# Value heads straight from the products: which operand is stationary in a two-layer diffusion step

## The chip, the cores and the metric

The kernel runs on one core of one Trainium2 chip. The metric is the time of one execution on the device in microseconds. TensorE is called PE in the profile, its weight loads PEld, VectorE DVE, ScalarE ACT, GpSimd POOL and the engine that issues most transfers SP.

## The reference, cut to what matters

Two trunk layers are applied to two groups of 128 tokens, context and latent, with model width 2048. Layer 0 mixes with eight latent (MLA) heads and eight grouped-query heads, layer 1 with eight differential heads; each layer ends in a gated feed-forward network. The change touches how the values of two kinds of heads are made:

```python
kv = (ckv_all @ w_kv_up).reshape(b, s, MLA_HEADS, MLA_NOPE_DIM + MLA_V_DIM)   # s = 128, or 128 cached + 128
...
va = kv[..., MLA_NOPE_DIM:]
out_a = softmax_attention(jnp.concatenate([qa_nope, qa_rope], axis=-1), ka, va, MLA_SCALE)
...
proj = h @ w_in                                                                # layer 1
v = proj[..., 2 * nq:].reshape(b, t, DIFF_HEADS, 2 * HEAD_DIM)
```

A latent head has 128 key and 128 value columns out of a latent of 512, for 384 token rows in all (context, cache, latent tokens). A differential head has two queries, two keys and one value of 256 columns, out of 2048 inputs, for 256 token rows; its cached values come from an input. All arithmetic is float32.

## The kernel before, in words

Activations lie with features on partitions and tokens along the free axis: `x` and the modulated input `hx` are tiles of 16 blocks of 128 features, each with 256 tokens (128 context, then 128 latent). Each input of a product is split into a high part rounded to float32r and the rest as a low part; `split` (L219 to L221) does that with a copy on ACT and a subtraction on DVE. A product is three matmuls for each block of 128 inputs: weight high by input high, weight high by input low, weight low by input high. In `gemm` (L304 to L318) the weight block, 128 inputs by 128 outputs, is the stationary operand, and the tokens move past it, 256 at once (384 in the latent heads' keys and values). The result has output features on partitions. It stands in one of three PSUM banks of the tag `acc`.

Weights come from memory in tiles of 1 MB named `raw`, 16 blocks of 128x128, three of them in turn. `Weights.chunk` (L255 to L281) loads a tile when its blocks have run out, splits each half of it into `wh` and `wl` of 1024 columns (four buffers each), and gives out the blocks of one chunk, that is of 128 outputs.

Attention needs the values the other way round, with tokens on partitions. So a value chunk is copied out of PSUM by ACT, transposed on PE by a matmul with the identity into a PSUM tile of the tag `att` (three of them in turn), and copied by ACT into the tile that the attention reads. For the differential heads that is L914 to L923 in `project`: two chunks, copied to `dev`, four transposes, two copies into `dv`. For the latent heads it is `vt` (L847), three transposes (L854) and `vm` (L855, L856) in `values_and_head`.

The order of the work. The tile framework orders each engine's queue by a simulated timeline, starting from the program's order; instructions marked with `keep_in_program_order` stay where they are. Attention is written as generators: `start` runs one to its first `yield`, and each `pump` runs every waiting one a step further (L147 to L158). `pump` also brings in the work on the modulation of later layers: rows of `w_ada`, as matmuls on PE (L427) or as sums on DVE (L404), at a rate for each stage. The first three products of a stage are made by `first_three` (L283 to L302); the next products take the entries of `todo`, the rest of one unit of modulation rows.

In the latent and grouped-query stage the loop at L825 goes over eight heads; every second one makes three query chunks for two heads. Each head starts a grouped-query head, makes a key chunk and a value chunk, and starts the latent head. In the differential stage `project` (L891 to L925) makes for each of eight heads two query chunks, two key chunks with rotation (L903 to L912; L909 on DVE and L905 to L907 on ACT read the accumulator), and two value chunks; `attend` (L927 to L976) then does scores (L934), softmax, transposes of the weights (L607), the weighted sum (L952 to L954), a norm (L958 to L968) and the turning back (L973). The output projection follows at L983.

## Time and profile before

| what | value |
|---|---|
| median of three runs | 2375.56 us (2375.53 to 2375.99) |
| the profiled execution's own time | 2375.77 us |
| its span, first to last instruction | 2374.0 us |
| mean granted TensorE clock | 0.989 |
| PE busy | 2315.6 us, 98% of the span |
| latent and grouped-query heads | about 223 to 375 us |
| differential heads | about 1208 to 1543 us |

The page of the profile has the busy time of each engine, the chain of work that ended last, and groups of instructions by source line. A row of a group reads: line, engine, operation, what it writes and reads, shape, count, then busy time in us and the mean of one in ns, and the idle time of the engine before it. A row of the timeline begins with the start in us and the duration; where instructions are merged, xN tells how many. Durations of matmuls overlap, so what one costs in a stream is read from the distance of the starts.

### The profile page before, as it was taken

How to read it: one execution, taken by the hardware profiler on the slowest of the kernel's cores; microseconds unless marked ns; L12 is line 12 of the kernel's file. 1: busy time of each engine (PE TensorE's matmuls, PEld its weight loads, DVE VectorE, ACT ScalarE, POOL GpSimd, SP SyncE). 2: the span in 40 equal slices, each digit the busy share in tenths (PEclk: the TensorE clock that was granted, in tenths of full speed). 3: DMA queues.
4: the chain of work that ended last, by engine and by line, in shares of the span. 5: the costliest groups of instructions: out<-in, count | busy, mean ns of one | idle time of the engine just before them, and what ended most of it. 6: DMA issues, size and time to landing. Idle time of an engine off the chain costs nothing.

```text
span 2374.0 us, 47094 instructions
## 1 busy us (share of the span) xinstructions
PE 2315.6 (98%) x19626; PEld 2196.9 (93%) x19626; DVE 1799.1 (76%) x2677; ACT 1172.7 (49%) x1855; POOL 136.6 (6%) x132
## 2 busy tenths in 40 slices
PE   8899999999999999999999999998999999999997
PEld 6778868799999999999989999897999999999997
DVE  2667544479999999999968889799899755666654
ACT  4345544365554345554465555445555434555542
POOL 0001001110000000001220000022000000000011
PEclk9999999999999999999999999998999999999998
DMA  9886677877767876777767788776677555555553
GB/s 378 353 342 241 238 266 300 309 275 266 261 252 281 296 277 251 265 264 268 300 229 256 267 315 290 269 288 240 247 260 260 207 195 195 196 194 192 192 192 120
DMA packets 92405, 610.81 MB, mean 257 GB/s; under 512 B 9952, under 2 KB 17824, under 8 KB 20512
## 3 DMA queue, kind: packets, MB, share of 16 engines
q1 hardware_dynamic: 92192, 607.80, 69.6%
q8 instruction: 154, 2.52, 0.4%
q14 instruction: 59, 0.48, 0.1%
HBM read 603.01 MB, written 4.75 MB: 256 GB/s over the span
## 4 chain that ended last, share of the span: by engine, by line
PE 95%; DVE 2%; DMA 1%; issue 1%; ACT 1%; POOL 0%; POOLq 0%; DVEq 0%; ACTq 0%
PE acc L313 28%; PE acc L317 28%; PE acc L314 28%; PE ada L427 3%; DMA araw<-w_ada 1%; PE att L617 1%; PE acc L300 1%; PE acc L299 1%; PE acc L301 1%; PE misc L427 0%; PE att L934 0%; PE att L607 0%; DVE wl L221 0%; PE ada L340 0%; PE ada L376 0%
## 5 line engine op out<-in xcount | busy, mean ns | idle before, releaser
L220 ACT CAST wh<-raw 128x1024 fp32r<-128x1024 f32 (+1 forms) x788 | 794.0, 1013 | 943.1 <-PE acc L314 775.7
L221 DVE TENSOR_TENSOR wl<-raw,wh 128x1024 fp32r<-128x1024 f32 (+1 forms) x788 | 923.0, 1186 | 343.8 <-ACT wh L220 324.5
L313 PE MATMUL acc<-hx,wh 128*128 128x256 f32 x4064 | 1131.6, 279 | 9.7 <-ACT wh L220 4.2
L317 PE MATMUL acc<-hx,wl 128*128 128x256 f32 x4064 | 1127.8, 278 | 0.7 <-DVE wl L221 0.7
L314 PE MATMUL acc<-hx,wh 128*128 128x256 f32 x4064 | 1128.4, 278 | 0.0
L313 PEld LDWEIGHTS acc<-hx,wh 128*128 128x128 f32 x4064 | 764.7, 188 | 35.7 <-issue 13.3
L317 PEld LDWEIGHTS acc<-hx,wl 128*128 128x128 f32 x4064 | 765.0, 188 | 8.9 <-issue 6.7
L314 PEld LDWEIGHTS acc<-hx,wh 128*128 128x128 f32 x4064 | 765.3, 188 | 7.4 <-issue 6.9
L404 DVE CUSTOM_DVE_ANT_0 junk<-araw,condb 128x2048 f32<-128x2048 f32 (+1 forms) x184 | 424.8, 2309 | 1.1 <-DMA araw<-w_ada 1.1
L314 PE MATMUL acc<-g,wh 128*128 128x256 f32 x1408 | 388.3, 276 | 0.0
L317 PE MATMUL acc<-g,wl 128*128 128x256 f32 x1408 | 388.0, 276 | 0.0
L313 PE MATMUL acc<-g,wh 128*128 128x256 f32 x1408 | 387.8, 276 | 0.0
L314 PEld LDWEIGHTS acc<-g,wh 128*128 128x128 f32 x1408 | 264.3, 188 | 0.0
L317 PEld LDWEIGHTS acc<-g,wl 128*128 128x128 f32 x1408 | 264.2, 188 | 0.0
L313 PEld LDWEIGHTS acc<-g,wh 128*128 128x128 f32 x1408 | 264.1, 188 | 0.0
L175 POOL TENSOR_TENSOR sqacc<-sqacc,sq 128x256 f32<-128x256 f32 x62 | 80.7, 1302 | 1584.3 <-issue 1290.8
L1011 ACT ACTIVATE cv<-acc,convw 128x256 f32<-128x256 f32 x176 | 98.3, 559 | 2.8 <-PE acc L301 2.8
L569 DVE SCALAR_TENSOR_TENSOR x<-acc,mod,x 128x128 f32<-128x128 f32 x192 | 58.0, 343 | 49.2 <-PE acc L317 49.2
L427 PE MATMUL ada<-araw,condw 128*32 128x512 f32 x608 | 83.2, 624 | 6.0 <-DMA araw<-w_ada 5.0
L1017 DVE SCALAR_TENSOR_TENSOR cv<-acc,convw,cv 128x254 f32<-128x254 f32 x176 | 84.4, 480 | 3.7
L1014 DVE SCALAR_TENSOR_TENSOR cv<-acc,convw,cv 128x254 f32<-128x254 f32 x176 | 83.7, 476 | 2.2 <-ACT cv L1011 2.2
L313 PE MATMUL acc<-oall,wh 128*128 128x256 f32 x208 | 58.4, 281 | 2.3 <-DVE x L569 2.3
(229 smaller groups left out, 1789.8 us busy)
## 6 DMA issues: line engine op xcount, KB each, us to landing
araw<-w_ada SPq DMA_DIRECT2D x186, 1024.0 KB, 5.4
raw<-w_up SPq DMA_DIRECT2D x176, 1024.0 KB, 4.8
raw<-w_down SPq DMA_DIRECT2D x88, 1024.0 KB, 4.8
raw<-w_in_c SPq DMA_DIRECT2D x48, 1024.0 KB, 5.5
raw<-w_in_ab SPq DMA_DIRECT2D x19, 1024.0 KB, 7.1
raw<-w_out_ab SPq DMA_DIRECT2D x16, 1024.0 KB, 7.1
raw<-w_out_c SPq DMA_DIRECT2D x16, 1024.0 KB, 5.3
raw<-w_ada SPq DMA_DIRECT2D x6, 1024.0 KB, 10.8
```

The source lines that it names most:

```text
L175: pool.tensor_tensor(out=st["acc"], in0=st["acc"], in1=sq, op=ALU.add)
L220: pin(act.copy(out_hi, src))
L221: pin(dve.tensor_tensor(out=out_lo, in0=src, in1=out_hi.bitcast(F32), op=ALU.subtract))
L313: fixed(pe.matmul(ps[:, :n], wh, xh(k), start=(i == 0), stop=False))
L314: fixed(pe.matmul(ps[:, :n], wh, xl(k), start=False, stop=False))
L317: fixed(pe.matmul(ps[:, :n], wl, xh(k), start=False, stop=(i == last)))
L404: tc.keep_in_program_order(dve.tensor_tensor_reduce(out=junk, in0=raw, in1=condb[:, c].rearrange("p (g n) -> p g n", g=4), scale=1.0, scal ...
L427: i = pe.matmul(ada["ps"][32 * g:32 * g + 32, :], condw[:, 4 * t + g, :], raw[:, g], start=(t == 0), stop=(t == 3), skip_group_check=True)
L569: dve.scalar_tensor_tensor(out=x[:, c, s], in0=ps[:, s], scalar=mod[:, l, 3 * which + 2, c, g:g + 1], in1=x[:, c, s], op0=ALU.mult, op1=AL ...
L1011: pin(act.activation(y, ps, AF.Identity, scale=cw[:, 1, m:m + 1], bias=cw[:, 3, m:m + 1]))
L1014: pin(dve.scalar_tensor_tensor(out=y3[:, :, 1:], in0=p3[:, :, :T - 1], scalar=cw[:, 0, m:m + 1], in1=y3[:, :, 1:], op0=ALU.mult, op1=ALU.add))
L1017: pin(dve.scalar_tensor_tensor(out=y3[:, :, :T - 1], in0=p3[:, :, 1:], scalar=cw[:, 2, m:m + 1], in1=y3[:, :, :T - 1], op0=ALU.mult, op1=A ...
```

## The change

`by_token` makes a product with the tokens stationary: the 128x128 block of the input, high or low part, is loaded as weights, and two chunks' weights, 256 columns, move past it. The result has tokens on partitions, which is what attention reads, and goes with one copy into the value tile.

For the differential heads, the two value chunks of a head are interleaved in memory so that each block of 128 inputs has its 256 columns side by side; `pairs` splits half a tile at a time, and two accumulators, one for each group of tokens, are filled together. For the latent heads, two heads go together: the tile of four chunks holds the two key chunks in its first half and the two value chunks, interleaved, in its second; the values of the pair come after both key chunks, in three runs over the three blocks of tokens. The two latent heads of a pair start after that, one `pump` apart. `values_and_head` is gone, and `vm` holds two heads.

```diff
--- before.py
+++ after.py
@@ -274,11 +274,34 @@
                     at = lo % 8 * P
                     wh, wl = wh_[:, at:at + w], wl_[:, at:at + w]
                     split(wh, wl, raw[:, lo * P:hi * P])
+                    self.pieces = (wh, wl)
                     for b in range(hi - lo):
                         s = slice(b * P, (b + 1) * P)
                         self.blocks.append((wh[:, s], wl[:, s]))
             out, self.blocks = self.blocks[:self.nblk], self.blocks[self.nblk:]
             return out
+
+        def pairs(self, lo):
+
+            if lo == 0:
+                self.raw = self.load()
+            wh = T_(wpool, [P, 1024], "wh", F32R, bufs=4)
+            wl = T_(wpool, [P, 1024], "wl", F32R, bufs=4)
+            split(wh, wl, self.raw[:, lo * P:(lo + 8) * P])
+            return wh, wl
+
+    def by_token(pieces, xs, outs, first, last):
+
+        wh, wl = pieces
+        n = len(xs)
+        for k in range(n):
+            a, b = first and k == 0, last and k == n - 1
+            s = slice(2 * k * P, (2 * k + 2) * P)
+            for (hi, lo), ps in zip(xs[k], outs):
+                pe.matmul(ps, hi, wh[:, s], start=a, stop=False)
+                pe.matmul(ps, lo, wh[:, s], start=False, stop=False)
+            for (hi, lo), ps in zip(xs[k], outs):
+                pe.matmul(ps, hi, wl[:, s], start=False, stop=b)
 
     def first_three(W, xh, xl, order, mid=None, fixed=False):
 
@@ -818,46 +841,47 @@
                 def mla(h, qnh, qrh, knh, vh):
                     half = slice(64 * (h % 2), 64 * (h % 2) + 64)
                     return head_ab(hp, [(qnh, knh), (qrh[half], kr[half])], rsm,
-                                   lambda b: vh[:, b], o, h)
+                                   lambda b: vh[:, b, h % 2], o, h)
 
                 flush()
                 start(gqa_query(0))
-                for h in range(8):
-                    if h % 2 == 0:
-                        for i in range(2):
-                            ps = gemm(WQ.chunk(), qh, qlo)
-                            qn[h + i] = T_(hp, [P, NT], "qn", bufs=4)
-                            act.copy(qn[h + i], ps)
-                            pump(RATE["heads"])
+                blocks = [slice(b * T, (b + 1) * T) for b in range(3)]
+                tokens = [[[(kv_in[:, k, 0, b], kv_in[:, k, 1, b])] for k in range(4)] for b in blocks]
+                for h in range(0, 8, 2):
+                    for i in range(2):
                         ps = gemm(WQ.chunk(), qh, qlo)
-                        ev = T_(tmp, [P, NT], "nt", bufs=4)
-                        act.copy(ev, ps)
-                        qr = T_(hp, [P, NT], "qr", bufs=2)
-                        act.copy(qr[:, 0:T], ev[:, 0:T])
-                        rope(qr[:, None, T:], ev[:, None, T:], 1, 32, "rcm", "rsm")
+                        qn[i] = T_(hp, [P, NT], "qn", bufs=4)
+                        act.copy(qn[i], ps)
                         pump(RATE["heads"])
-                    if h < 7:
-                        start(gqa_query(h + 1))
-                    start(gqa(h))
-                    ps = gemm(WK.chunk(), kh, klo, 3 * T)
-                    kn = T_(hp, [P, 3 * T], "kn", bufs=2)
-                    act.copy(kn, ps)
+                    ps = gemm(WQ.chunk(), qh, qlo)
+                    ev = T_(tmp, [P, NT], "nt", bufs=4)
+                    act.copy(ev, ps)
+                    qr = T_(hp, [P, NT], "qr", bufs=2)
+                    act.copy(qr[:, 0:T], ev[:, 0:T])
+                    rope(qr[:, None, T:], ev[:, None, T:], 1, 32, "rcm", "rsm")
                     pump(RATE["heads"])
-                    ps = gemm(WK.chunk(), kh, klo, 3 * T)
-                    vt = T_(hp, [P, 3 * T], "vt", bufs=2)
-                    act.copy(vt, ps)
+                    kn = []
+                    for i in range(2):
+                        if h + i < 7:
+                            start(gqa_query(h + i + 1))
+                        start(gqa(h + i))
+                        ps = gemm(WK.chunk(), kh, klo, 3 * T)
+                        kn.append(T_(hp, [P, 3 * T], "kn", bufs=2))
+                        act.copy(kn[i], ps)
+                        pump(RATE["heads"])
+                    wide = WK.pieces
+                    WK.blocks = []
+                    vm = T_(hp, [P, 3, 2, P], "vm", bufs=1)
+                    vs = vm.rearrange("p b i d -> p (b i d)")
+                    two, one = T_(pacc, [P, 512], "acc"), T_(pacc, [P, 512], "acc")
+                    for xs, out in zip(tokens, (two[:, :NT], two[:, NT:], one[:, :NT])):
+                        by_token(wide, xs, [out], True, True)
+                    act.copy(vs[:, :2 * NT], two)
+                    act.copy(vs[:, 2 * NT:], one[:, :NT])
                     pump(RATE["heads"])
-
-                    def values_and_head(h, vt, *a):
-                        pt = T_(ppool["att"], [P, 512], "att", bufs=3)
-                        for b in range(3):
-                            pe.transpose(pt[:, b * T:(b + 1) * T], vt[:, b * T:(b + 1) * T], ident)
-                        vm = T_(hp, [P, 3, P], "vm", bufs=2)
-                        act.copy(vm.rearrange("p b d -> p (b d)"), pt[:, :3 * T])
-                        yield
-                        yield from mla(h, *a, vm)
-
-                    start(values_and_head(h, vt, qn[h], qr, kn))
+                    start(mla(h, qn[0], qr, kn[0], vm))
+                    pump(RATE["heads"])
+                    start(mla(h + 1, qn[1], qr, kn[1], vm))
                 flush()
 
         ensure(l, 2)
@@ -911,16 +935,15 @@
                     dve.tensor_tensor(out=turned, in0=turned, in1=sh, op=ALU.subtract)
                     pump(rate)
             sp.dma_start(out=A["o_diff_k"][:, 2 * h:2 * h + 2], in_=k[:, :, 0:T])
-            pt = T_(ppool["att"], [P, 512], "att", bufs=3)
-            for i in range(2):
-                ev = T_(cp, [P, NT], "dev", bufs=2)
-                act.copy(ev, product())
-                pump(rate)
-                for g in range(2):
-                    pe.transpose(pt[:, g * NT + i * P:g * NT + (i + 1) * P],
-                                 ev[:, g * T:(g + 1) * T], ident)
-            act.copy(v[:, 0], pt[:, 0:NT])
-            act.copy(v[:, 2], pt[:, NT:])
+            ps = [T_(pacc, [P, 512], "acc")[:, :NT] for _ in range(2)]
+            at = [slice(g * T, (g + 1) * T) for g in range(2)]
+            for k0 in range(0, KD, 4):
+                xs = [[(hx[:, k0 + j, t], hx[:, k0 + j, NT:2 * NT][:, t]) for t in at] for j in range(4)]
+                by_token(W.pairs(2 * k0 % 16), xs, ps, k0 == 0, k0 == 12)
+                if k0 % 8:
+                    pump(rate)
+            act.copy(v[:, 0], ps[0])
+            act.copy(v[:, 2], ps[1])
             sp.dma_start(out=A["o_diff_v"][:, h], in_=v[:, 0])
             return q, k, v
 
@@ -1186,10 +1209,15 @@
     for h in range(0, 8, 2):
         parts += [w[:, h, :128], w[:, h + 1, :128], w[:, h, 128:], w[:, h + 1, 128:]]
     a["w_q_up"] = _blocks(np.concatenate(parts, 1), range(12), 2)
-    a["w_kv_up"] = _blocks(i["w_mla_kv_up"][0], range(16), 4)
+    w = _blocks(i["w_mla_kv_up"][0], range(16), 4).reshape(4, P, 2, 2, 4, P)
+    a["w_kv_up"] = np.stack([w[:, :, :, 0].reshape(4, P, 1024),
+                             w[:, :, :, 1].transpose(0, 1, 3, 2, 4).reshape(4, P, 1024)], 2).reshape(4, P, 2048)
     a["w_out_ab"] = _blocks(i["w_out_ab"][0], range(16), 1)
     order = [b + 2 * h + j for h in range(8) for b in (0, 16, 32) for j in range(2)]
     a["w_in_c"] = _blocks(i["w_in_c"][0], order, 1)
+    w = a["w_in_c"].reshape(8, 6, P, KD, P)
+    v = w[:, 4:].transpose(0, 2, 3, 1, 4).reshape(8, P, 2, 2048).transpose(0, 2, 1, 3)
+    a["w_in_c"] = np.concatenate([w[:, :4].reshape(8, 4, P, 2048), v], 1).reshape(48, P, 2048)
     a["w_out_c"] = _blocks(i["w_out_c"][0], range(16), 1)
     order = [b + m for m in range(NFF) for b in (0, NFF)]
     a["w_up"] = np.stack([_blocks(i["w_ffn_up"][l], order, 1) for l in range(NL)])
```

## The prediction

> **What bounds the kernel now.** I read the page first: which engine is busy, and of which engine the chain that ended last is made.
>
> ```profile
> PE 2315.6 (98%) x19626; PEld 2196.9 (93%) x19626; DVE 1799.1 (76%) x2677; ACT 1172.7 (49%) x1855; POOL 136.6 (6%) x132
> PE 95%; DVE 2%; DMA 1%; issue 1%; ACT 1%; POOL 0%; POOLq 0%; DVEq 0%; ACTq 0%
> ```
>
> TensorE (PE) is busy 98% of the span and makes up 95% of the chain, so an instruction that leaves PE shortens the run, and one that leaves ScalarE (ACT, 49%) does not. Whether this holds in the two stages that change, the busy time by windows says: the latent heads (223 to 375 us), the differential heads (1240 to 1510), the end of that stage (1510 to 1549), and two stretches of plain products for scale.
>
> ```profile
> core 0: us, PE busy (x) PEld busy (x) DVE busy (x) ACT busy (x) POOL busy (x), PEclk, DMA share, GB/s
> 223.00:375.00 152.00, 149.61 (x1046) 115.38 (x1049) 72.76 (x212) 76.80 (x178) 5.66 (x8) 1.00 0.68 255
> 484.00:1195.00 711.00, 711.00 (x6265) 707.14 (x6265) 646.15 (x816) 358.66 (x473) 27.48 (x17) 1.00 0.73 271
> 1240.00:1510.00 270.00, 270.00 (x2285) 264.22 (x2284) 240.02 (x365) 147.15 (x306) 6.05 (x6) 1.00 0.78 279
> 1510.00:1549.00 39.00, 32.48 (x229) 25.36 (x228) 24.63 (x41) 16.47 (x36) 1.38 (x2) 0.91 0.74 274
> 1560.00:1620.00 60.00, 60.00 (x512) 60.00 (x511) 60.00 (x71) 26.55 (x37) 11.84 (x11) 1.00 0.76 279
> ```
>
> In the differential heads PE has no idle time at all, in the latent heads 152.0 - 149.6 = 2.4 us. Only the end of the differential stage is slack: 39.0 - 32.5 = 6.5 us idle, and a granted clock of 0.91, which is 0.09 x 39 = 3.5 us more; 10 us in all. The plain stretches give the pitch of a matmul of 256 columns: 711/6265 = 113.5 ns in one, 60/512 = 117.2 ns in the other. The granted clock is 1.00 in both, so the kernel has two pitches, a short and a long one.
>
> **The products themselves.** For a differential head the count stays: before, 2 chunks x 16 k x 3 matmuls = 96 of 256 columns; after, 16 k x 2 token blocks x 3 = 96 of 256. What is stationary is still a 128x128 float32r block, one weight load for each matmul as before (x19626 on both). No row shows activations stationary and weights moving; shapes and types are equal, so I take equal pitch. The bounds are the two pitches above: 768 matmuls x 3.7 ns = 2.8 us either way. That the new order goes from one accumulator to another and back costs nothing by this place, where three matmuls of L299 in a row (the loop there goes over three accumulators) keep 0.34 us for three:
>
> ```profile
> 479.17 0.50 PE L299 MATMUL acc<-hx,wh 128*128 128x256 f32 x3
> 479.51 0.28 PE L300 MATMUL acc<-hx,wh 128*128 128x256 f32 x1
> ```
>
> For the latent heads 8 x 4 x 3 = 96 matmuls of 384 columns become 4 pairs x 3 token blocks x 4 x 3 = 144 of 256: the same columns, 48 instructions more. The timeline gives the wide ones:
>
> ```profile
> 257.20 0.33 PE L313 MATMUL acc<-kv_in,wh 128*128 128x384 f32 x1
> ...
> 258.41 0.34 PE L314 MATMUL acc<-kv_in,wh 128*128 128x384 f32 x1
> 258.59 0.39 PE L631 MATMUL att<-pT,vm 128*128 128x128 f32 x2
> ```
>
> Eight from 257.20 to 258.59 is 174 ns each, 96 x 174 = 16.7 us; 144 x 113.5 to 117.2 = 16.3 to 16.9 us. I take +0.1 us, bounds -0.4 and +0.2. The Trainium skill speaks against this part: "TensorE: Matmul & The Clock Gate", section Back-to-back issue gap, gives about 81 ns for a matmul of 128 columns in a stream and 131 ns for 512, which is a large fixed part; a straight line between them (an estimate from that page) makes 96 x 114 = 11.0 us into 144 x 98 = 14.1 us, 3.1 us lost. The trace does not agree: 174 to about 115 is the ratio of the columns, so the fixed part is near nothing.
>
> **The transposes.** This is the gain. The groups by line, with shapes kept apart:
>
> ```profile
> L920 PE MATMUL att<-cst,dev 128*128 128x128 f32 x32 | 5.9, 272 | 0.0
> L917 ACT COPY dev<-acc 128x256 f32<-128x256 f32 x16 | 5.8, 366 | 0.0
> L854 PE MATMUL att<-cst,vt 128*128 128x128 f32 x24 | 4.0, 277 | 0.0
> L848 ACT COPY vt<-acc 128x384 f32<-128x384 f32 x8 | 3.8, 480 | 0.8 <-PE acc L317 0.8
> L856 ACT COPY vm<-att 128x384 f32<-128x384 f32 x8 | 3.8, 480 | 2.3 <-PE att L854 2.2
> L369 ACT COPY am<-ada 128x512 f32<-128x512 f32 x20 | 11.7, 587 | 24.2 <-PE ada L427 24.1
> ```
>
> All 56 transposes go. Their 272 ns is a duration, and matmuls overlap, so the price is how far the next product is pushed back:
>
> ```profile
> 1246.17 0.28 PE L314 MATMUL acc<-hx,wh 128*128 128x256 f32 x1
> 1246.29 0.38 PE L920 MATMUL att<-cst,dev 128*128 128x128 f32 x2
> 1246.42 0.37 PE L317 MATMUL acc<-hx,wl 128*128 128x256 f32 x1
> 1246.62 0.28 PE L313 MATMUL acc<-hx,wh 128*128 128x256 f32 x1
> 349.27 0.49 PE L854 MATMUL att<-cst,vt 128*128 128x128 f32 x3
> 349.60 0.82 PE L617 MATMUL att<-kg,qb 128*128 128x128 f32 x4
> ```
>
> From 1246.17 to 1246.62 PE does two products (0.23 us) and two transposes: 0.22 us for the two. 16 such pairs: 3.5 us. Three L854 hold the next work from 349.27 to 349.60, 0.33 us; 8 times: 2.6 us. The sum is -6.1 us. The Trainium skill ("TensorE: Matmul & The Clock Gate", section Part 4: PE-mode transpose) gives about 275 ns for one within a kernel; as a duration the row agrees (272), but counted so the sum would be 56 x 0.275 = -15.4 us, and the starts in the timeline, 0.11 us apart, refute that.
>
> **Copies, queues, waits.** ACT loses 16 x 0.37 + 16 x 0.48 = 13.6 us of copies and gains 4 x (0.59 + 0.37) = 3.8 us, counted at nothing: PE is what is full. DVE, POOL, SP and the DMAs keep their work: each head still fetches two 1 MB tiles, and the pumps are as many. In head 0 the second entry of `todo` (four transposes L376) moves from the first value product to the next head's first query product; its modulation columns are first read in the output projection, after 1547 us, and its buffer by no one sooner: nothing.
>
> The new wait: both value accumulators are taken from the start of the value product, so the second one, which held the first key product (three banks in turn, six products a head), must have been read one product (5.4 us) sooner than now. Behind that matmul the whole PE queue stands. The last reader is L909 on DVE; the tightest head I found is the last:
>
> ```profile
> 1496.56 2.29 DVE L404 CUSTOM_DVE_ANT_0 junk<-araw,condb 128x2048 bf16<-128x2048 f32 x1
> 1498.97 0.28 DVE L909 TENSOR_TENSOR dk<-acc,cst 128x128 f32<-128x128 f32 x1
> 1500.56 0.26 ACT L905 COPY dsh<-acc 64x128 f32<-64x128 f32 x1
> ```
>
> One of the sums for the modulation (L404, 2.29 us) already goes ahead of it. L909 is done at 1499.25; the value product can start only when the second key product has ended, which L905 marks at 1500.56. 1.3 us are left: nothing, with a risk priced below.
>
> **The end of the differential stage.** Each head uses three PSUM tiles of the tag `att` in turn; the value transposes held one from the first of them to the copies. After, a head takes five instead of six. In the last head this matters:
>
> ```profile
> 1506.32 0.28 DVE L911 TENSOR_TENSOR dk<-dk,dsh 128x128 f32<-128x128 f32 x1
> 1512.40 0.37 ACT L917 COPY dev<-acc 128x256 f32<-128x256 f32 x1
> 1519.73 0.87 DVE L966 SCALAR_TENSOR_TENSOR on<-att,var,cst 128x256 f32<-128x256 f32 x2
> 1523.12 0.60 PE L920 MATMUL att<-cst,dev 128*128 128x128 f32 x4
> 1523.88 0.82 PE L934 MATMUL att<-dk,dq 128*128 128x128 f32 x4
> 1525.69 0.82 PE L934 MATMUL att<-dk,dq 128*128 128x128 f32 x4
> 1532.71 1.94 PE L427 MATMUL ada<-araw,condw 128*32 128x512 f32 x8 [2.19 <-DMA araw<-w_ada]
> 1548.13 0.36 PE L313 MATMUL acc<-oall,wh 128*128 128x256 f32 x1 [2.35 <-DVE x L569]
> ```
>
> The keys are ready at 1506.6 and the last value chunk was copied at 1512.8, yet the scores L934 run at 1523.9 and 1525.7, behind L920 and the transposes of the head before, while PE burns the output matmuls that could have hidden the softmax. Then it waits 2.19 us for a transfer, and 2.35 us more before 1548.13. With the tile free the scores can run up to 11 us sooner, and part of the 10 us lost there returns. Bounds: 0 (the order stays, or the transfer L427 waits for holds the end anyhow) and -10; below nothing is possible too, a new order may leave PE idle longer, and I give that -4 to +4 as a rival. I take -4, nearer the lower end since one of the waits is a transfer.
>
> **Sum.** -6.1 + 0.1 - 4 = -10.0 us. The profiled execution took 2375.77 us, a span of 2374.0 and 1.8 around it; the median of the runs is 2375.56, 0.2 less, so the trace stands for the runs. Forecast: 2365.6 us.
>
> **Rivals.** About 0.2%, 4.8 us, is what a measurement of this kernel can tell from no change.
>
> 1. Only the transposes count, or the ends of the two stages eat some of them: idle there is small and the order of the queues changes. -6.1 alone is 2369.5; with up to 4 us given back, 2373.5. The former is still faster, the latter the same.
> 2. The transposes were hidden, nothing is gained: 2375.6. For it would speak idle PE around them; the window 1240 to 1510 shows 270.00 busy of 270.00. Unlikely.
> 3. Slower by the pitch. It changes within the differential stage too:
>
> ```profile
> 1270.00:1283.00 13.00, 13.00 (x112) 13.00 (x112) 13.00 (x18) 6.08 (x11) 0.00 (x0) 1.00 0.87 283
> 1290.00:1308.00 18.00, 18.00 (x161) 18.00 (x160) 17.50 (x28) 12.26 (x28) 0.00 (x0) 1.00 0.80 299
> ```
>
> That is 116 and 112 ns (a matmul at the edge counts whole), with transposes and scores between the two stretches. So I read it as a choice that each break in the stream makes and that lasts until the next; it filled 1560 to 1620. The two feed-forward stages have hardly a break, and the first is short throughout (6265 matmuls). If the shifted start makes one of them fall into the long pitch, it costs 6265 x 3.7 ns = 23 us: 2388.8. It decides from the last break before that stage; against it speaks that this break is not touched by the change. The same thing to a gain: 1560 to 1620 in the short pitch is worth 512 x 3.7 ns = 1.9 us.
> 4. Slower by the accumulator: if the sums on DVE (2.29 us each) come before L909, its 1.3 us are gone and PE stands for 2.29 - 1.3 = 1.0 us in a head, 8 us over eight: 2373.6. It takes two such sums in every head, 26 us, to be slower: 2392.
>
> **Chances.** The forecast with the end of the stage partly recovered 0.50; rival 1 0.30, half of it on each side of 4.8 us; rival 2 0.04; rival 3 0.06; rival 4 with a worse end of a stage 0.10, mostly slower. Faster by over 0.2% 0.65, within 0.2% 0.20, slower 0.15. The range goes down by the whole 10 us of the end of the stage with some pitch, to 2356, and up over rival 1 and part of rival 4 to 2378.
>
> **What would show it.** No L920, L854, L917 and L848 groups; PE at 19626 - 56 + 48 = 19618 instructions, ACT at 1855 - 32 + 8 = 1831. Eight heads from first to last value product shorter by 3.5 us with PE still at 100%. The value matmuls at 113 to 118 ns apart: 130 or more would refute the equal pitch. In the last head, L934 before 1515 us and the idle time of the end of the stage down from 6.5: if the scores still follow the output matmuls, the -4 is wrong. A wait of PE at the second value accumulator, released by DVE L909, would be rival 4. Feed-forward stretches with 6000 matmuls at 117 ns would be rival 3.

## The result, and the profile after

The changed kernel takes 2373.28 us (median of 21 runs; 2375.59 us before in the same session): ratio 0.9985, interval 0.9979 to 0.9991, or 3.6 us (2.1 to 5.0) less. The two medians alone are 2.3 us apart, which is inside that interval. The forecast was 10.0 us less. The profiled execution has a span of 2372.4 us against 2374.0.

The page of the changed kernel: busy time, and the engines on the chain that ended last.

```profile
PE 2313.5 (98%) x19618; PEld 2193.2 (92%) x19618; DVE 1798.5 (76%) x2677; ACT 1163.1 (49%) x1831; POOL 140.1 (6%) x132
PE 93%; DVE 3%; DMA 2%; ACT 1%; issue 1%; POOL 0%; POOLq 0%; DVEq 0%; ACTq 0%
```

The instructions are as counted (PE 19618, ACT 1831). PE's busy time fell by only 2.1 us, and on the chain PE gave two points to VectorE and transfers. The windows say where; they are those of the prediction, read over the changed kernel.

```profile
core 0: us, PE busy (x) PEld busy (x) DVE busy (x) ACT busy (x) POOL busy (x), PEclk, DMA share, GB/s
223.00:375.00 152.00, 149.19 (x1081) 113.84 (x1083) 74.10 (x214) 74.66 (x172) 7.22 (x8) 1.00 0.69 255
1240.00:1510.00 270.00, 270.00 (x2266) 264.21 (x2265) 240.58 (x367) 144.97 (x295) 4.99 (x6) 1.00 0.77 278
1510.00:1549.00 39.00, 31.92 (x200) 23.61 (x199) 24.62 (x40) 11.90 (x29) 3.29 (x2) 0.83 0.74 273
484.00:1195.00 711.00, 711.00 (x6269) 708.72 (x6265) 643.74 (x811) 358.47 (x472) 26.67 (x16) 1.00 0.74 271
```

The feed-forward stage is still short (6269 matmuls in 711 us). PE is full in the differential heads, as before, but gets fewer instructions done than the shorter list allows. The end of the stage, where 4 us were to be won, got worse: a granted clock of 0.83 instead of 0.91, and 7.1 us idle instead of 6.5.

By stages, from landmarks that both kernels have (first copy of a latent query; first residual of the first layer; first and last copy of the rotation, L905; first residual of the second layer), as means of two traces of each kernel (the second ones are the last experiment):

| stretch | before | after | difference | forecast |
|---|---|---|---|---|
| latent heads, to the first residual | 148.9 | 146.9 | -2.0 | -2.5 |
| first projection and feed-forward, to the first L905 | 854.1 | 853.5 | -0.7 | 0 |
| differential heads, first to last L905 | 272.3 | 271.3 | -1.0 | -3.5 |
| end of the stage, last L905 to first residual | 46.6 | 48.8 | +2.2 | -4 |
| from there to the end | 826.6 | 824.5 | -2.1 | 0 |

The stretch ahead of the first is equal (225.9 us). The differences add up to -3.6 us. The rest of the work is to explain the third and fourth row.

**The third row: the pitch.** The value matmuls are L301, L302 and L304. Two stretches of the timeline of the changed kernel, one where a value product follows an ordinary one (L336, L337, L340), and one in the last head:

```profile
1306.69 0.28 PE L336 MATMUL acc<-hx,wh 128*128 128x256 f32 x1
...
1307.25 0.28 PE L340 MATMUL acc<-hx,wl 128*128 128x256 f32 x1
1307.37 0.28 PE L301 MATMUL acc<-wh,hx 128*128 128x256 f32 x1
1307.48 0.28 PE L302 MATMUL acc<-wh,hx 128*128 128x256 f32 x1
1307.59 0.28 PE L304 MATMUL acc<-wl,hx 128*128 128x256 f32 x1
...
1307.93 0.28 PE L304 MATMUL acc<-wl,hx 128*128 128x256 f32 x1
...
1499.76 0.28 PE L301 MATMUL acc<-wh,hx 128*128 128x256 f32 x1
1499.88 0.28 PE L302 MATMUL acc<-wh,hx 128*128 128x256 f32 x1
...
1500.70 0.28 PE L304 MATMUL acc<-wl,hx 128*128 128x256 f32 x1
```

From 1306.69 to 1307.93 eleven gaps take 1.24 us: 113 ns each, ordinary and swapped alike. From 1499.76 to 1500.70 eight take 0.94 us: 117.5 ns each. So swapped operands can run at the short pitch. In two of the eight heads the product ahead is short, and there the value product starts short and turns long at its first break; in a third head the last 18 gaps, behind a break, are short; nearly all else is long. For the whole stage, take the gap from the start of each 256-column product of the heads to the next start on PE, from 1226 to 1510 us, and call it short up to 115 ns and long from 116 to 121: of 2106 gaps 785 are long before, of 2121 gaps 1346 after. Of the gaps inside value products, 664 of 721 are long.

**The fourth row: the scores.** The timeline at the end of the stage, changed kernel (of the head before the last, L632 copies the softmax weights out of an `att` tile, L989 reads its output tile for the last time, L996 is the turning back; L957 are the scores of the last head, L630 the transposes of its softmax; L450 modulation rows):

```profile
1509.95 0.49 ACT L632 COPY pT<-att 128x384 f32<-128x384 f32 x1
...
1518.84 0.87 DVE L989 SCALAR_TENSOR_TENSOR on<-att,var,cst 128x256 f32<-128x256 f32 x2
...
1522.30 0.27 PE L996 MATMUL att<-cst,on 128*128 128x128 f32 x1
1522.41 0.82 PE L957 MATMUL att<-dk,dq 128*128 128x128 f32 x4
1523.07 0.49 PE L996 MATMUL att<-cst,on 128*128 128x128 f32 x3
1523.39 0.82 PE L957 MATMUL att<-dk,dq 128*128 128x128 f32 x4
...
1530.74 1.06 PE L450 MATMUL ada<-araw,condw 128*32 128x512 f32 x8 [2.00 <-DMA araw<-w_ada]
1531.73 0.55 PE L630 MATMUL att<-cst,p 128*128 128x128 f32 x3
...
1533.22 1.94 PE L450 MATMUL ada<-araw,condw 128*32 128x512 f32 x8 [0.94 <-DMA araw<-w_ada]
...
1538.96 1.94 PE L450 MATMUL ada<-araw,condw 128*32 128x512 f32 x8 [0.94 <-DMA araw<-w_ada]
```

The scores run at 1522.4, not before 1515: right behind the first transpose of L996. It was not for want of a tile. The tiles of the scores of the head before had been read by 1493.7 us and that of its softmax transposes by 1510.4, so from there to 1522.3 two of the three `att` tiles stood empty; only the head's output stood in one, until 1519.7. What follows has no products left to hide it, waits for rows of `w_ada`, and from 1533 on runs at half the clock (the same eight matmuls of L450 take 1.94 us instead of 1.06).

### The profile page after: what moved, and what is told of

It reads as the page before. It is cut to its first block, busy times and chain, and to the rows that moved or that the text cites. A ratio compares the mean times of both kernels' runs of the same rounds, so it can differ in the third digit from the quotient of the medians.

```text
span 2372.4 us, 47058 instructions
## 1 busy us (share of the span) xinstructions
PE 2313.5 (98%) x19618; PEld 2193.2 (92%) x19618; DVE 1798.5 (76%) x2677; ACT 1163.1 (49%) x1831; POOL 140.1 (6%) x132
## 4 chain that ended last, share of the span: by engine, by line
PE 93%; DVE 3%; DMA 2%; ACT 1%; issue 1%; POOL 0%; POOLq 0%; DVEq 0%; ACTq 0%
PE acc L336 26%; PE acc L340 26%; PE acc L337 26%; PE ada L450 3%; PE acc L302 2%; PE acc L301 2%; PE acc L304 1%; DMA araw<-w_ada 1%; PE att L640 1%; DVE wl L221 1%; PE acc L323 1%; PE acc L324 1%; DVE nt L539 0%; PE acc L322 0%; PE misc L450 0%
## 5 line engine op out<-in xcount | busy, mean ns | idle before, releaser
L336 PE MATMUL acc<-hx,wh 128*128 128x256 f32 x3808 | 1058.7, 279 | 9.5 <-ACT wh L220 4.2
L340 PE MATMUL acc<-hx,wl 128*128 128x256 f32 x3808 | 1056.8, 278 | 0.5 <-DVE wl L221 0.5
L337 PE MATMUL acc<-hx,wh 128*128 128x256 f32 x3808 | 1056.6, 278 | 0.0
L336 PEld LDWEIGHTS acc<-hx,wh 128*128 128x128 f32 x3808 | 716.4, 188 | 33.6 <-issue 12.6
L340 PEld LDWEIGHTS acc<-hx,wl 128*128 128x128 f32 x3808 | 716.5, 188 | 10.7 <-issue 8.7
L337 PEld LDWEIGHTS acc<-hx,wh 128*128 128x128 f32 x3808 | 717.5, 188 | 8.0 <-issue 7.5
L337 PE MATMUL acc<-g,wh 128*128 128x256 f32 x1408 | 388.3, 276 | 0.0
L340 PE MATMUL acc<-g,wl 128*128 128x256 f32 x1408 | 388.0, 276 | 0.0
L336 PE MATMUL acc<-g,wh 128*128 128x256 f32 x1408 | 387.8, 276 | 0.0
L337 PEld LDWEIGHTS acc<-g,wh 128*128 128x128 f32 x1408 | 264.3, 188 | 0.0
L340 PEld LDWEIGHTS acc<-g,wl 128*128 128x128 f32 x1408 | 264.1, 188 | 0.0
L336 PEld LDWEIGHTS acc<-g,wh 128*128 128x128 f32 x1408 | 264.0, 188 | 0.0
L450 PE MATMUL ada<-araw,condw 128*32 128x512 f32 x608 | 84.1, 624 | 7.3 <-DMA araw<-w_ada 5.9
L302 PE MATMUL acc<-wh,hx 128*128 128x256 f32 x256 | 68.5, 281 | 0.0
```

The lines of the kernel that those rows point to most:

```text
L302: pe.matmul(ps, lo, wh[:, s], start=False, stop=False)
L336: fixed(pe.matmul(ps[:, :n], wh, xh(k), start=(i == 0), stop=False))
L337: fixed(pe.matmul(ps[:, :n], wh, xl(k), start=False, stop=False))
L340: fixed(pe.matmul(ps[:, :n], wl, xh(k), start=False, stop=(i == last)))
L450: i = pe.matmul(ada["ps"][32 * g:32 * g + 32, :], condw[:, 4 * t + g, :], raw[:, g], start=(t == 0), stop=(t == 3), skip_group_check=True)
```

## The experiments

Each experiment is named by its label. Its ratio is to the kernel before in the same session.

**e1_no_turn: the kernel before without the 56 transposes.** The weights stay stationary. The value chunks are copied straight from PSUM into the attention's tile, so the values that it reads are not turned; the transposes and their second copies are left out. Shown are the differential heads; the latent ones read `vt` in the same way.

```diff
-            pt = T_(ppool["att"], [P, 512], "att", bufs=3)
             for i in range(2):
-                ev = T_(cp, [P, NT], "dev", bufs=2)
-                act.copy(ev, product())
+                ps = product()
+                act.copy(v[:, 0:3:2, i * P:(i + 1) * P], ps.rearrange("p (g t) -> p g t", g=2))
                 pump(rate)
-                for g in range(2):
-                    pe.transpose(pt[:, g * NT + i * P:g * NT + (i + 1) * P],
-                                 ev[:, g * T:(g + 1) * T], ident)
-            act.copy(v[:, 0], pt[:, 0:NT])
-            act.copy(v[:, 2], pt[:, NT:])
```

> The kernel before, weights stationary everywhere, with the 56 transposes and the copies behind them left out (the values then stand the wrong way round; that part of the computation is left out). It separates the loss of the breaks from the exchange of the operands. Theory A (operands): products with activations stationary and weights moving fall into the long pitch, 117 to 118 ns, and that gave back 2 to 3 us of the 6.1. Then here, with the operands as before, the value products are as often in the short pitch as the other products, the differential stage is 3.5 us shorter from the first to the last query and key products of the heads, and the time is about 2369.5 (6 us under before). Theory B (breaks): the transposes were breaks after which PE often took the short pitch; without them the long one stays, whoever is stationary. Then the value products are at 117 ns here too, the stage is about 1 us shorter, and the time is that of the changed kernel, 2372.

Measured: 0.9972 (0.9961 to 0.9983), 6.6 us less. The differential heads take 269.3 us, 3.0 less, with 921 long gaps, 136 more than before, which at 4.2 ns each cost 0.6 us; so the transposes there were worth some 3.6 us. The latent stretch is 2.2 us shorter. So the price of the transposes in the sum, 6.1 us, is about right, and the changed kernel loses some of it by other means. That the whole run agrees with it so well is partly luck: the rest of the 6.6 us comes from stretches without such transposes. The end of the stage takes 47.8 us: without the transposes it is no shorter either.

**e2_diff and e3_latent: the change in one kind of head alone.** e2 leaves the latent heads as they were, e3 the differential ones.

> The change in the differential heads alone; latent heads as before. Both theories of the pitch: in the differential stage 3.5 us less of transposes and some 2.4 us more of long pitch, so about 1 us less, 2374.5; the value products at a mean duration of 281 ns. If the whole is the sum of its parts, this and the run of the latent part alone lie together 3.5 us under before.

> The change in the latent heads alone; differential heads as before. Transposes 2.6 us less, the 48 more instructions in the long pitch 0.2 to 0.6 more: the first residual of the output projection 1.5 to 2.5 us earlier, the time 2373 to 2374. If a wait in the latent heads took the rest, its idle time shows before 375 us.

Measured: 0.9990 (0.9981 to 0.9999) and 0.9989 (0.9979 to 0.9999), so each half is worth some 2.5 us, too close to no change to divide finely by times alone. The traces divide it: e3 has the latent stretch 2.1 us shorter (146.8 us) and the differential one as before (272.6); e2 has the latent one as before (148.5) and the differential one 1.3 us shorter (271.0), with 1295 long gaps of 2129.

**e5_misc: the changed kernel with one tile moved.** The turning back of a head's output takes the single PSUM bank `misc` in place of one of the three `att` tiles.

```diff
-            pt = T_(ppool["att"], [P, 512], "att", bufs=3)
+            pt = bank()
             for i in range(2):
                 for g in range(2):
                     pe.transpose(pt[:, i * NT + g * T:i * NT + (g + 1) * T],
```

> The changed kernel, with the turning back of a differential head's output (L996) in the PSUM tile of the tag misc in place of att, so that the next head's scores no longer stand behind it in the turn of the att tiles. Theory (order of the tiles): the last head's scores waited for that, not for the value transposes; they run at about 1511 us instead of 1522, the end of the differential stage loses up to 6 us of idle time and half clock, the time is 2366 to 2370. Rival (transfer): the end waits for the modulation rows of PE anyway; scores earlier, but the first residual of the output projection at 1548 as before and the time 2372.

Measured: 0.9962 (0.9950 to 0.9974), 9.0 us less than before. Its timeline:

```profile
1508.12 1.47 PE L957 MATMUL att<-dk,dq 128*128 128x128 f32 x8
...
1513.79 0.27 PE L996 MATMUL misc<-cst,on 128*128 128x128 f32 x1
...
1525.55 0.49 PE L630 MATMUL att<-cst,p 128*128 128x128 f32 x3
```

The scores now run 14 us sooner, ahead of the turning back, and the transposes of the softmax (L630) 6 us sooner. The head before the last had already gained: its softmax transposes start at 1499.0 us, 9.9 sooner. The end of the stage takes 40.5 us instead of 49.9. What had held the scores was the turning back of the head before, which takes its `att` tile ahead of them in the program's order; it was not the value transposes, which both kernels lack. How that order gets into PE's queue, by the turn in which the pool hands out its tiles or by the simulated timeline, these runs do not separate.

**e6_before_misc: the same line in the kernel before.**

> The kernel before with one line changed: the turning back of a head's output takes the single bank `misc` instead of the tile `att`. Theory 'order of the att tiles': the scores of the last head stood behind the turning back of the head before it, with the values made either way, so the same 5 to 6 us come back without the change: ratio 0.9975, scores of the last head before 1512 us instead of 1523.9. Rival 'both needed': the value transposes hold the tiles as well (six a head, now five with the copies in the way), so the scores stay behind at over 1518 us and the ratio is 0.9990 or more.

Measured: 0.9973 (0.9961 to 0.9984), 6.4 us less, without the change. The time is that of the first theory, the scores lie between the two: they still share the tiles with the value transposes, and half of them come late:

```profile
1514.56 0.81 PE L934 MATMUL att<-dk,dq 128*128 128x128 f32 x4
...
1520.92 0.27 PE L973 MATMUL misc<-cst,on 128*128 128x128 f32 x1
...
1521.60 0.82 PE L934 MATMUL att<-dk,dq 128*128 128x128 f32 x4
```

The end of the stage, last L905 to first residual, by windows of the kernel before, the changed one, e1, and this one:

```profile
1500.60:1547.40 46.80, 41.01 (x305) 33.86 (x303) 32.38 (x50) 19.35 (x42) 1.38 (x2) 0.93 0.75 277
```

```profile
1498.10:1548.10 50.00, 42.92 (x297) 34.61 (x296) 34.73 (x54) 17.01 (x39) 3.29 (x2) 0.88 0.71 262
```

```profile
1496.40:1544.20 47.80, 40.07 (x302) 32.83 (x300) 34.64 (x54) 17.43 (x39) 3.29 (x2) 0.96 0.72 274
```

```profile
1502.70:1540.50 37.80, 35.65 (x286) 31.60 (x285) 27.26 (x42) 15.36 (x37) 1.38 (x2) 1.00 0.70 261
```

With the scores ahead, PE is idle for 2.2 us instead of 5.8 and the clock stays at 1.00. Of the 9 us that the stretch lost, 2.5 come back later: from the first residual to the end this kernel takes 829.1 us, the one before 826.6.

**e4_shift: the value weights at another place in memory.** By the program's allocation (the traces hold no addresses), activations start at 224 bytes modulo 256 and weights at 32, in all kernels so far. Here all buffers of `wh` and `wl` are widened, and the value weights lie 192 bytes further into theirs, at 224 as well; only this is shown.

```diff
-            wh = T_(wpool, [P, 1024], "wh", F32R, bufs=4)
-            wl = T_(wpool, [P, 1024], "wl", F32R, bufs=4)
+            wh = T_(wpool, [P, 1088], "wh", F32R, bufs=4)[:, 48:48+1024]
+            wl = T_(wpool, [P, 1088], "wl", F32R, bufs=4)[:, 48:48+1024]
```

> The changed kernel with the value weights of the differential heads 192 bytes further into a wider wh/wl buffer (1088 columns instead of 1024), so that the moving operand of the value products starts at the same place within 256 bytes as the activations do when they move. Theory 'place': the long pitch of the value products (664 of 721 gaps at 117.5 ns) belongs to where the moving operand lies; then most of them go to 113.3 ns, the differential stage from the first to the last L905 is 2 to 3 us shorter (271.3 to about 269), and the run about 2.4 us faster than the changed kernel, ratio to before 0.9975. Theory 'operands swapped': what matters is that the activations are stationary, wherever they lie; the counts stay, the ratio stays near 0.9985 and the stage at 271.3.

Measured: 0.9991 (0.9982 to 1.0000). The place does count, but the guess of the good place was wrong: the value matmuls take neither pitch but a third one.

```profile
1282.74 0.28 PE L301 MATMUL acc<-wh,hx 128*128 128x256 f32 x1
...
1283.94 0.28 PE L301 MATMUL acc<-wh,hx 128*128 128x256 f32 x1
```

Ten gaps in 1.20 us are 120 ns each; of 710 value gaps up to 121 ns, 707 are above 115. The ordinary products of the same stage keep the two old pitches.

**e7_mirror: another order inside the value products.**

```diff
-        for k in range(n):
-            a, b = first and k == 0, last and k == n - 1
-            s = slice(2 * k * P, (2 * k + 2) * P)
-            for (hi, lo), ps in zip(xs[k], outs):
-                pe.matmul(ps, hi, wh[:, s], start=a, stop=False)
-                pe.matmul(ps, lo, wh[:, s], start=False, stop=False)
-            for (hi, lo), ps in zip(xs[k], outs):
-                pe.matmul(ps, hi, wl[:, s], start=False, stop=b)
+        for j, ps in enumerate(outs):
+            for k in range(n):
+                hi, lo = xs[k][j]
+                s = slice(2 * k * P, (2 * k + 2) * P)
+                pe.matmul(ps, hi, wh[:, s], start=first and k == 0, stop=False)
+                pe.matmul(ps, hi, wl[:, s], start=False, stop=False)
+                pe.matmul(ps, lo, wh[:, s], start=False, stop=last and k == n - 1)
```

> The changed kernel with another order inside the value products: for each block of tokens by itself, input high by weight high, input high by weight low, input low by weight high, so that the stationary block is the same in two matmuls of three, as in the other products, and the accumulator changes only every 12 matmuls. Theory 'order': the long pitch comes from the accumulators in turn or from a stationary block that is never the same twice; then most value matmuls go from 117.5 to 113.3 ns, the differential stage from 271.3 to about 269 us and the ratio to 0.9975. Theory 'operands swapped' or 'place': the pitch stays long for most, the ratio near 0.9985.

Measured: 0.9980 (0.9971 to 0.9989), 433 of 722 value gaps long instead of 664 of 721. Neither expectation holds: most stay long, but far fewer. e5, which does not touch the products at all, has 461 of 714. So the order inside the product is not shown to be the cause; the share moves without it.

**e8_place128 and e9_place64: e5 with two other places of the value weights.** As in e4, with 32 and 16 columns in place of 48, and the `misc` line of e5.

> The changed kernel with the turning back of the output in the bank `misc`, and with the value weights 128 bytes further into a wider buffer: within 256 bytes the moving operand then lies 192 bytes behind the stationary one, as in the ordinary products (it lay 64 behind in the changed kernel, at the same place in the one with 192 bytes, where the value matmuls went at 120 ns). Theory 'relative place': what counts is where the two operands of a matmul lie to each other; then the value matmuls take the long pitch as seldom as the ordinary products of the kernel before (785 of 2106, some 40%, against 461 of 715 with the `misc` bank alone), the differential stage from first to last L905 is near 269.5 us, and the ratio to before 0.9955. Rival 'each break draws': the long pitch depends on the matmul that the PE queue lands on after a break; then the share stays above 55% or moves with no order, no gap of 120 ns either way, ratio 0.996 to 0.997.

> The same with 64 bytes instead of 128: the moving operand of the value products lies 128 bytes behind the stationary one within 256. Theory 'relative place': a distance other than nought is free of the 120 ns; the share of the long pitch differs from that with 128 bytes. Rival 'each break draws': the two kernels differ by chance only, in the same 55 to 70%. Ratio to before 0.9955 to 0.997.

Measured: 0.9953 (0.9940 to 0.9967) and 0.9972 (0.9962 to 0.9983). With 128 bytes 392 of 710 value gaps are long (55%, not the 40% expected); ten gaps of it,

```profile
1282.76 0.28 PE L301 MATMUL acc<-wh,hx 128*128 128x256 f32 x1
...
1283.89 0.28 PE L304 MATMUL acc<-wl,hx 128*128 128x256 f32 x1
```

take 1.13 us, 113 ns each. So they can be short, but the pitch need not wait for a break to change: in all eight heads of e8 it turns within the first five matmuls of the value product, from long to short in four and from short to long in the other four. One of the latter:

```profile
1460.15 0.28 PE L340 MATMUL acc<-hx,wl 128*128 128x256 f32 x1
...
1460.95 0.28 PE L301 MATMUL acc<-wh,hx 128*128 128x256 f32 x1
...
1461.54 0.28 PE L304 MATMUL acc<-wl,hx 128*128 128x256 f32 x1
```

Seven gaps take 0.80 us, the next five 0.59: 114 and 118 ns. With 64 bytes the mean of the value gaps is 118.7 ns (116.2 in e5, 115.9 with 128 bytes, 119.9 in e4_shift), in a pattern of mostly 115 to 122 that sets in also where the product ahead was short; so another distance than nought does not by itself give the two old pitches. e8 is the fastest kernel here, 2366.7 us against 2376.9 before; its interval overlaps that of e5, so what the place adds to it is not shown by the times.

**e10_all_shift: e4_shift for all weights.** The edit is shown against e4_shift; `halves` has the same.

```diff
-            wh = T_(wpool, [P, 1088], "wh", F32R, bufs=4)[:, :1024]
+            wh = T_(wpool, [P, 1088], "wh", F32R, bufs=4)[:, 48:48+1024]
...
-                        wh_ = T_(wpool, [P, 1088], "wh", F32R, bufs=4)[:, :1024]
+                        wh_ = T_(wpool, [P, 1088], "wh", F32R, bufs=4)[:, 48:48+1024]
```

> The changed kernel with all weights of all products 192 bytes further into a wider buffer, not only the value weights of the differential heads: in every float32r product stationary and moving operand then lie at the same place within 256 bytes. Theory 'relative place': the ordinary products of 256 columns leave 113.3 and 117.5 ns for 120 ns too, in the two feed-forward stages as well, which are short now; about 18,000 matmuls by 6 ns are 90 to 110 us, ratio to before 1.037 to 1.046, and PE is as full. Rival 'only swapped products feel it' (what suffers is an activation as the stationary operand at that place): the ordinary products stay, ratio 0.999 as with the value weights alone.

Measured: 1.0406 (1.0389 to 1.0424), 2474.0 us, 96 us more, inside the expected 90 to 110. The window of the first feed-forward stage:

```profile
484.00:1195.00 711.00, 711.00 (x5897) 705.23 (x5897) 618.21 (x787) 340.40 (x458) 19.12 (x15) 1.00 0.70 256
```

5897 matmuls in the time of 6269, 120.4 ns in the mean of their gaps, clock 1.00. So ordinary products feel it too: with this shift, which by the allocation puts both operands at the same place modulo 256, nearly all gaps of that stage are 120 ns. e4 has the same wider buffers and its ordinary products keep their pitch, so it is the shift and not the width. That 256 bytes is the period was not tested.

**e11_after_again and e12_before_again: both kernels once more, for a second trace.**

> The changed kernel as it is, for a second trace of it. If each break in the stream draws the pitch anew in each execution, the value matmuls have another share of the long one than 664 of 721 and the stretches change from long to short at other places; if the pitch follows from the program alone, the same stretches are long. For the end of the differential stage: from the last L905 to the first residual of the output projection it took 49.9 us in the first trace of the changed kernel and 46.8 in that of the kernel before; the theory that the order of the `att` tiles holds the scores expects 46 to 50 again, with the scores of the last head behind 1518 us; the forecast's -4 us would be 43.

> The kernel before as it is, for a second trace of it: how far pitch and stage lengths differ between two executions of one program. The first had 785 of 2106 gaps in the differential stage at the long pitch, 272.3 us from the first to the last L905, and 46.8 us from there to the first residual. Drawn anew: the count moves by more than 100 and the length by up to 2 us; following from the program: counts within 50, lengths within 0.5 us.

Measured: the ratios are 0.9983 (0.9973 to 0.9994) and 1.0005 (0.9965 to 1.0044; one of these eight executions took 2404.6 us, which widens it). In the differential heads the pitch follows from the program: 664 of 721 value gaps long again, 1356 long of 2120 in all (1346 of 2121), 271.33 us (271.32); before, 788 of 2102 (785 of 2106) and 272.34 us (272.33). The end of the stage took 47.6 and 46.3 us (49.9 and 46.8), the scores of the changed kernel came at 1521.3. Behind the transfers' waits the pitch is not fixed: the output projection of the kernel before, long in the first trace, is short in the second.

```profile
1560.00:1620.00 60.00, 60.00 (x531) 60.00 (x531) 60.00 (x71) 27.33 (x39) 11.95 (x11) 1.00 0.75 275
```

That changed nothing in the length of the stage. From its first residual to its last, in the first trace and in the second:

```profile
1547.40:1625.80 78.40, 74.01 (x626) 73.72 (x626) 78.40 (x96) 34.07 (x48) 16.61 (x14) 0.99 0.73 269
```

```profile
1548.20:1626.60 78.40, 72.96 (x626) 72.70 (x626) 78.40 (x97) 33.96 (x48) 16.44 (x14) 0.96 0.74 271
```

VectorE is busy 78.40 of 78.40 us there, PE is not, so a shorter pitch buys nothing.

**The kernels together.** If the pitch is what the differential heads lost, then their length is 272.3 us, less 3.5 where the transposes are out, plus 4.2 ns (117.5 less 113.3) for each long gap over the 785 of before:

| kernel | long gaps | by this sum | measured | end of the stage | ratio |
|---|---|---|---|---|---|
| e1, transposes out | 921 of 2145 | 269.4 | 269.3 | 47.8 | 0.9972 |
| e2, differential alone | 1295 of 2129 | 271.0 | 271.0 | 48.4 | 0.9990 |
| e3, latent alone | 866 of 2105 | 272.7 | 272.6 | 46.9 | 0.9989 |
| changed kernel | 1346 of 2121 | 271.2 | 271.3 | 49.9 | 0.9985 |
| e7, mirrored order | 1193 of 2130 | 270.5 | 271.0 | 46.4 | 0.9980 |
| e5, `misc` | 1148 of 2105 | 270.4 | 270.5 | 40.5 | 0.9962 |
| e8, `misc` and place | 995 of 2117 | 269.7 | 270.0 | 38.1 | 0.9953 |
| e6, before with `misc` | 683 of 2071 | 271.9 | 271.8 | 37.8 | 0.9973 |

Seven of the eight agree within 0.3 us, e7 within 0.5. e4, e9 and e10 are not in the table because their value matmuls run at other pitches. The kernels with `misc` (e9 too) have ends of 38 to 41 us, all others 46 to 50.

## Why the prediction was wrong

The direction held, the size did not: -3.6 us, where -10.0 was forecast; the median lies in the range and just inside rival 1 (2369.5 to 2373.5), whose place it describes: the transposes count, and the ends and the pitch eat some of it. That it came out there is partly luck: two stretches that the sum had at nothing, the second and the last row of the table by stages, gave 2.8 of the 3.6 us, and the three stretches that the change touches gave 0.8. The prediction took 4.8 us for the least that can be told from no change; with 21 runs the interval reaches 1.5 us to either side.

**The end of the stage, -4 us: the step that failed.** The prediction said that with the tile of the value transposes free the scores could run up to 11 us sooner. The tile was free and the scores ran at 1522.4 and 1521.3 (1523.9 before). The step took the wait for one for a free tile. But two of the three tiles were empty, and the turning back of the head before, which comes first in the program's order, stood ahead of the scores. The lines that it quoted showed this already: the value transposes L920 of the last head start only at 1523.12, so until then they had held no tile, and the scores of L934 at 1523.88 stand behind two things, L920 and "the transposes of the head before", of which it took the first for the cause. e5 shows that it was the second, and e6 shows it for the first half of the scores. The measured term is +2.2 us (+3.1 and +1.3 against the trace of the same order), with each trace's share of half clock in it. That the end got longer rather than staying equal isn't settled: in e1, e2, e4, e7 and the two traces of the changed kernel, where the value transposes of the differential heads are out, it took 46.4 to 49.9 us, and with them (e3 and the two traces before) 46.3 to 46.9.

**The pitch, 0 with bounds of 2.8 us: mis-sized.** Swapped operands can run at the same pitch, as the prediction assumed and the rows at 1306.69 show. But it took the share of long stretches for unchanged. 561 more gaps became long: 561 x 4.2 ns = 2.4 us in the differential heads, and 98 of 114 gaps of the latent value matmuls, 0.4 us. It lies near the upper end of the bounds that were given for it. Why so many more are long is not shown: the share moves when one tile moves (e5), when the order inside the product changes (e7) and with the operands' place (e8), and no run tells what sets it. The reading of rival 3, a pitch that lasts from one break to the next, holds in the changed kernel, though not in e8; but it struck the changed stage and not a feed-forward one. And its gain, 1.9 us for a short pitch from 1560 to 1620, is not there: the second trace of the kernel before has that pitch, and its output projection is no shorter.

**The transposes, -6.1 us: right.** e1 gives 6.6 us (4.0 to 9.3) for the whole run; its trace gives 3.6 us for the differential heads once the long gaps are counted and 2.2 us for the latent ones, 5.8 in all.

**The latent matmuls, +0.1 us: right.** The latent heads gained 2.0 us, that is -2.5 and the 0.4 us of the pitch. By the estimate from the Trainium skill in the prediction ("TensorE: Matmul & The Clock Gate", section Back-to-back issue gap) they would have lost half a microsecond, 3.1 against the 2.6 of the transposes; the traces do not agree.

**The other rivals.** The accumulator never held PE: in all eight heads the first value matmul starts 113 to 131 ns behind the last product. Counting copies, pumps and DMAs at nothing fits the differential heads, where PE is busy 270.00 of 270.00 us, and the latent ones, where it is idle 2.8 us instead of 2.4. The 2.1 us between the first residual of the second layer and the end were in no part of the sum. They came in e1, e2 and e4 too (824.3 us), not in e3 (827.3) nor e7 (826.9); 1.5 of them lie between the output projection and the feed-forward stage, where in the first traces the granted clock was 0.89 after and 0.77 before. What sets that was not tried.

## What to carry to other kernels

Before crediting a freed buffer to a waiting instruction, check that it lacked a buffer at all: here two of three were empty, and what it stood behind was an earlier user of the same pool whose own data were late. Moving that one tile to another bank was worth 6.4 us with the work unchanged, against 3.6 for the whole rewrite. Where PE is full, read a stream's pitch from the starts of its matmuls and count how many run at each; a change of order can change the share, and 4 ns times a stage's matmuls can eat the gain. Where operands swap their roles, look at where both lie in memory: with both at the same place modulo 256 bytes the matmuls here were slower.

## What the runs showed of the hardware

A stream of float32r matmuls of 256 columns showed three pitches at full clock. With the operands 64 bytes (changed kernel) or 192 bytes (ordinary products, e8) apart modulo 256, by the allocation, it takes 113.3 or 117.5 ns, and mostly keeps what it has until the next break, except where e8 goes from an ordinary to a value product; at the same place it takes 120.4 ns in the mean of the first feed-forward stage (e10), 96 us over the kernel; at 128 bytes 118.7 in the mean (e9). Which of the two pitches a stretch takes was repeated in both traces of the differential heads, where PE is busy without a gap from 1240 to 1510 us, and changed in the output projection, which follows waits for transfers. Why the distance counts is not shown.

At the end of the differential stage, in the first trace of the changed kernel, PE went to half its clock although its longest wait there was 2.0 us. The mean clock of 0.83 over 39 us is about 13 us at half. The Trainium skill ("TensorE: Matmul & The Clock Gate", section What's actually happening) lets the clock fall after an idle window of some 3.4 us; here no single wait was that long, only several close together, 2.0 and 0.94 us ahead of 1533. Whether these set it off is not shown.
